# A hybrid decoder layer: the memory queries of the second token half by pair, and the memory splits ahead of the token scaling

## The chip, the cores and the metric

The kernel runs on one core of one Trainium2 chip. The metric is the device time of one execution in microseconds. PE is the TensorE, ACT the ScalarE, DVE the VectorE, POOL the GpSimd, and SP the SyncE, which here only issues DMAs. Each engine works through its own queue in order.

## The reference

One decoder layer for 1024 tokens of width 1024, all in float32:

```python
h = rmsnorm(x, norm_g)
pool_v, pool_gate, sb_q, sb_k, sb_v, sb_gate, mem_q, mem_gate = split(h @ w_in)
y_pool = pool_mixer(pool_v, pool_w, pool_scale) * silu(pool_gate)      # 256 wide
y_sb = stick_breaking_attention(sb_q, sb_k, sb_v) * silu(sb_gate)      # 8 heads of 64
mem_k, mem_v = split(rmsnorm(mem, mem_norm_g) @ w_mem_kv)              # 256 memory tokens
y_mem = memory_attention(mem_q, mem_k, mem_v) * silu(mem_gate)         # 4 heads of 64
out = x + concat(y_pool, y_sb, y_mem) @ w_out

def memory_attention(q, mem_k, mem_v):
    q, mem_k = rmsnorm(q, q_norm_g), rmsnorm(mem_k, k_norm_g)          # per head
    p = softmax(q @ mem_k.T * 64 ** -0.5)
    return p @ mem_v
```

## The kernel before

Every float32 operand of a matmul is held as a high part (a copy in a shorter format, made by ACT) and a low part (the rest, a subtraction on DVE or POOL), and each product is three matmuls: high by high, high by low, low by high. The normalised tokens, transposed, are `hh[k]` and `hl[k]` for eight blocks k of 128 channels; a projection of 128 output columns (a unit) takes eight steps of three 128x512 matmuls for each half of the tokens (th 0 and 1), so 16 steps. Its weights (512 KB) come into the one raw buffer `wr`, ACT makes the high part (L148), POOL the low part in four pieces (L152), and the two buffers `wh` and `wl` hold two units' weights each. The next unit's weights are asked for at the first step of a unit (`chain`, L227).

PE's order is the program's order throughout. Up to `start.close()` (L923) the order on ACT, DVE and POOL is the program's order too; behind it a planner in the compiler orders these three, by its own cost estimates. SP's order is the planner's everywhere.

The start. The memory (256 tokens, tiles `mt`) and its key/value weights come first. `m_evac(kk)` splits two blocks of the transposed memory, `kv_split(kk)` splits a quarter of the key/value weights, half of the low part on DVE and half on POOL (L158), and `kv_step(kk)` multiplies them on PE. Between them lie the first four token tiles: `square` on ACT, `root` (an operation on DVE and a power on POOL, L123), `newton` and `scale` on DVE (L127 to L133). `mn[i].root()` is the same for the two memory tiles, whose scales are needed only later, by `kv_evac`. `warm` issues transposes that nobody reads. `h_step(th, k)` then transposes block k of four token tiles on PE and splits it into `hh[k]` on ACT (L381) and `hl[k]` on DVE (L382).

The memory queries (two units, pr 0 and 1, of two heads each) are the first units. `half[pr, th]` are the eight steps of one half. Half 0 of both pairs runs step by step in turn, together with the last `h_step`s; then comes half 0 of the first stick-breaking query unit `u_q[0]`, with the evacuations `mq_late` of the memory queries between its steps; then half 1 of both pairs, in turn. In this last block also lie: `kv_root` and `kv_newton`, which normalise the memory keys into `kmn` (squares on ACT, a sum on DVE, a power on POOL, four small operations and two products on DVE); `mem_ss(pr, th)`, which sums the squares of the queries by head on PE (L551, 128x2 results) and copies them out on DVE; `mem_scale(th)`, which makes of them the queries' scale factors (with a power of 16 columns on POOL, L95); and `km_step(kmn, pr)`, which transposes the keys on PE (L469) and splits them into `km`, four copies on ACT (L476) and four differences on DVE (L481).

An evacuation of a query unit is two copies on ACT and two differences on DVE (L256 to L259); a memory query unit has a third ACT operation, the squares (L543).

Behind `start.close()` PE runs half 1 of `u_q[0]` and the first step of the key unit `u_k[0]`, and then `weave`, which lays the steps of memory attention (`mem_main`) between the steps of the following units by estimated costs. One item of `mem_main` is: scores on PE (L574, bank `z`), row maximum and its scaling on DVE (L576, L580), two exponentials on ACT (L584), reciprocal on DVE, scaling half on POOL and half on DVE (L595), transposes (L493) and the product with the values (L512) on PE. `weave` runs again for the four stick-breaking attentions, and the output projection ends the kernel.

A value unit (`v_unit`) evacuates each half into the one buffer `vt` (ACT L295, DVE L298), and `late(th)` transposes it on PE (L306) and splits it into `V_v`. `chain` puts `late(0)` among the unit's own steps, and `late(1)` among those of the next unit.

Of the kernel before, what the change touches and what calls it, by code (L numbers as in the profile page):

```python
# [17 lines left out]
KD = D // P  # L18
# [7 lines left out]
def layer_kernel(  # L26
# [31 lines left out]
    def ps(tag, name):  # L58
        return psum.tile([P, 512], F32, tag=tag, name=name, bufs=banks[tag])
# [75 lines left out]
    def load_raw(src, name, raw=None):  # L135
        raw = slot("wr", f"wr_{name}") if raw is None else raw
        nc.sync.dma_start(raw[:], src)
        return raw
# [26 lines left out]
    def run(steps):  # L165
        for _, fn in steps:
            fn()
# [59 lines left out]
    def chain(units, after=None):  # L227
        steps, rest = [], []
        for n, u in enumerate(units):
            nxt = units[n + 1] if n + 1 < len(units) else after  # L230
            a = list(u.steps)
            if nxt is not None:
                a[0] = (KC, lambda f0=a[0][1], nxt=nxt: (f0(), nxt.weights()))
            if u.late is not None:
                a = a[:10] + u.late(0) + a[10:]
            steps += a[:2] + rest + a[2:]
            rest = u.late(1) if u.late is not None else []
        return steps + rest

# [102 lines left out]
    mn = [Norm(mt[i][:], f"m{i}") for i in range(2)]  # L342
# [6 lines left out]
    def warm(dst, n):  # L349
        for i in range(n):  # L350
            nc.tensor.transpose(dst[:, 0:P], ident[:], ident[:])
# [38 lines left out]
    def m_evac(kk):  # L390
        tps = [(2 * kk + j, tm[kk][:, j * M : (j + 1) * M]) for j in range(2)]
        for k, tp in tps:
            nc.scalar.activation(mh[:, k, :], tp, AF.Identity, scale=gcol[:, 8 + k : 9 + k])
        for k, tp in tps:
            nc.vector.scalar_tensor_tensor(
                ml[:, k, :], tp, gcol[:, 8 + k : 9 + k], f(mh[:, k, :]), op0=ALU.mult, op1=ALU.subtract
            )
# [3 lines left out]
    def kv_split(kk):  # L401
        tags = (("wh", "wl"), ("wh", "wl"), ("qa0", "qb0"), ("KA0",))[kk]
        w_kv.append(split_w(raw_kv[kk], f"kv{kk}", tags, (nc.vector, nc.gpsimd)))

    def kv_step(kk):
        wh, wl = w_kv[kk]
        for j in range(2):
            k = 2 * kk + j
            wc = slice(j * 512, (j + 1) * 512)
            for w, m in ((wh, mh), (wh, ml), (wl, mh)):  # L410
                for i in range(2):
                    nc.tensor.matmul(
                        kvp[i][:],
                        m[:, k, i * P : (i + 1) * P],
                        w[:, wc],
                        start=(k == 0 and m is mh and w is wh),
                        stop=(k == KD - 1 and w is wl),
                    )

    kvs, kmn, k_root = [], [], []  # L420
# [134 lines left out]
    def mem_scale(th):  # L555
        c = slice(16 * th, 16 * th + 16)
        r = rsqrt_cols(ssb[:, c], 16, 1.0 / HD, f"q{th}")()
        nc.vector.tensor_scalar_mul(qsc[:, c], r[:], HD**-0.5)
# [245 lines left out]
    m_evac(0)  # L804
    kv_split(0)
    m_evac(1)
    for i in range(2):
        mn[i].root()
    kv_step(0)
    xn[0].square()  # L810
    xn[0].root()
    kv_split(1)
    xn[0].newton()
    xn[0].scale(nc.vector)
    m_evac(2)
    kv_step(1)
    xn[1].square()
    xn[1].root()
    kv_split(2)
    xn[1].newton()  # L820
    xn[1].scale(nc.vector)
    xn[2].square()
    xn[2].root()
    m_evac(3)
    kv_step(2)
    kv_split(3)
    xn[2].newton()
    xn[3].square()
    xn[3].root()
    xn[2].scale(nc.vector)  # L830
    kv_step(3)
    raw_mq = [load_raw(w_in_v[:, :, 2560 + pr * P : 2560 + (pr + 1) * P], f"mq{pr}", early_raw[4 + pr]) for pr in range(2)]
    for i in range(4, 8):
        nc.sync.dma_start(xt[i][:], xv[i * P : (i + 1) * P, :])
    xn[3].newton()
    xn[3].scale(nc.vector, slice(0, 512))
    warm(ps("tr", "warm"), 8)
    w_mq = [(slot("wh", f"wh_mq{pr}", dt=F32R), slot("wl", f"wl_mq{pr}", dt=F32R)) for pr in range(2)]
    wc = (slice(0, 512), slice(512, 1024))

# [3 lines left out]
    def mq_low(pr, c, eng):  # L844
# [7 lines left out]
    mq_low(1, wc[0], nc.gpsimd)  # L852
    mq = [mem_q(pr) for pr in range(2)]
    half = {
        (pr, th): unit_half(lambda pr=pr: w_mq[pr], f"mq{pr}", th, mq[pr][1], late_h=False) for pr in range(2) for th in range(2)
    }
    h_step(0, 0)
    mq_high(1, wc[1])
# [51 lines left out]
            mq_late[pr][n]()  # L910
    for k in range(KD):
        half[0, 1][k][1]()
        half[1, 1][k][1]()
        if k == 0:
            kv_root()
            kv_newton()
        if k in (2, 3):
            mem_ss(k - 2, 0)
        if k == 4:
            mem_scale(0)  # L920
        if k in (5, 6):
            km_step(kmn, k - 5)
    start.close()  # L923
    fill = u_q[0].steps[8:] + chain([u_k[0], u_v[0], u_v[1], u_g[0], u_q[1], u_k[1], u_g[1]], u_q[2])
    cut = 8 + 16 + 17 + 17 + 16
    fill, fill_0 = fill[:cut], fill[cut:]
    run(fill[:9])
    y_mem = [slot(f"Y{pr}", f"y_mem{pr}") for pr in range(2)]

    def mem_late(n):  # L930
        mem_ss(n, 1)
        if n == 1:
            mem_scale(1)

    fill[13:13] = [(0.45, lambda: mem_late(0))]
    fill[16:16] = [(0.45, lambda: mem_late(1))]
    weave(mem_main(mq, y_mem), fill[9:], 4, 1.0)

    def attn(p):
# [225 lines left out]
```

## Time and profile before

| | |
|---|---|
| time, median of 3 runs (lowest to highest) | 532.24 us (531.69 to 532.82) |
| the profiled execution: its time, its span | 533.07 us, 531.3 us |
| PE busy | 515.5 us, 97% of the span |
| DVE, ACT, POOL busy | 392.6, 286.7, 178.9 us (74, 54, 34%) |
| DMA | 37.25 MB, mean 70 GB/s |
| mean granted clock of PE | 0.99 |

The span goes from the first to the last instruction of the one profiled execution; all times of rows are microseconds from its start. Idle time of an engine counts only where PE comes to wait for it. The granted clock is told as a share of the full level: 1.00 is 2.4 GHz and 0.5 is 1.2 GHz.

### The profile page before, as it was taken

To read this page: it belongs to the slowest core of one execution; us is meant where nothing else is said; L and a number is where in the kernel's file an instruction comes from. 1 tells how busy PE (TensorE), PEld (TensorE's weight loads), DVE (VectorE), ACT (ScalarE), POOL (GpSimd) and SP (SyncE) were. 2 spreads that over 40 slices of the span, in tenths; PEclk is the share of its full clock that TensorE was granted. 3 is DMA by queue.
4 is the path that set the end of the run, shared out by engine and by line. 5 is a ranking of instruction groups with operands and counts; after the bars stand their busy time and mean duration, and the time that the engine had idled before them with its cause. 6 is when DMAs were issued, how large, how long until landed. Compare 5 with 4: busy or idle time off the path is not lost.

```text
span 531.3 us, 7462 instructions
## 1 busy us (share of the span) xinstructions
PE 515.5 (97%) x2724; PEld 431.9 (81%) x2724; DVE 392.6 (74%) x635; ACT 286.7 (54%) x549; POOL 178.9 (34%) x196
## 2 busy tenths in 40 slices
PE   7899979999999999999999999999999999999997
PEld 6587858888788888888888888888788888888886
DVE  3877555776667885877666777657988859999973
ACT  7687454766756555555545654545544539462400
POOL 4770445542322021022202211222345920034790
PEclk9999987999999999999999999999999999999999
DMA  8911012310110230113011113100110415413123
GB/s 316 320 44 41 0 41 74 86 35 6 41 39 1 80 81 0 41 49 93 20 39 41 41 40 80 39 16 26 41 41 0 159 42 197 159 41 119 40 110 128
DMA packets 37244, 37.25 MB, mean 70 GB/s; under 512 B 1990, under 2 KB 26840, under 8 KB 37208
## 3 DMA queue, kind: packets, MB, share of 16 engines
q1 hardware_dynamic: 37208, 36.78, 22.1%
q8 instruction: 21, 0.34, 0.3%
q14 instruction: 15, 0.12, 0.1%
HBM read 28.39 MB, written 4.19 MB: 61 GB/s over the span
## 4 chain that ended last, share of the span: by engine, by line
PE 83%; DVE 6%; ACT 5%; issue 2%; DMA 2%; POOL 1%; SPq 0%; DVEq 0%; ACTq 0%; POOLq 0%
PE av L512 7%; PE z L640 6%; PE ta L493 6%; PE u_g L209 5%; PE u_k L209 5%; PE u_v L209 5%; PE u_q L209 4%; PE u_mg L209 3%; PE oS L1047 3%; PE oS L1049 3%; PE u_g L206 3%; PE oS L1048 3%; PE u_pv L209 3%; PE u_k L206 3%; PE u_v L206 3%; PE u_mq L209 2%
## 5 line engine op out<-in xcount | busy, mean ns | idle before, releaser
L648 DVE TENSOR_TENSOR_SCAN be<-be,later 128x128 f32<-128x128 f32 (+3 forms) x64 | 92.1, 1454 | 14.4 <-ACT be L644 13.5
L498 ACT ACTIVATE ah<-ta,mone 128x512 fp32r<-128x512 f32 (+1 forms) x80 | 51.6, 645 | 58.3 <-PE ta L493 57.5
L499 DVE SCALAR_TENSOR_TENSOR al<-ta,ah 128x512 fp32r<-128x512 f32 (+1 forms) x80 | 50.7, 633 | 24.6 <-ACT ah L498 23.8
L644 ACT ACTIVATE be<-z 128x128 f32<-128x128 f32 (+3 forms) x96 | 45.5, 490 | 31.0 <-PE z L640 29.4
L493 PE MATMUL ta<-ident,be 128*128 128x128 f32 x288 | 44.9, 273 | 0.1
L493 PEld LDWEIGHTS ta<-ident,be 128*128 128x128 f32 x288 | 34.9, 140 | 8.0 <-DVE be L648 0.7
L512 PEld LDWEIGHTS av<-ah,V_v 128*128 128x128 f32 x160 | 29.7, 188 | 6.7
L512 PE MATMUL av<-al,V_v 128*128 128x256 f32 (+1 forms) x160 | 31.7, 280 | 1.1 <-DVE al L499 1.1
L512 PE MATMUL av<-ah,V_v 128*128 128x256 f32 (+1 forms) x160 | 30.3, 271 | 0.0
L152 POOL TENSOR_TENSOR wl_k<-wr_k,wh_k 128x256 fp32r<-128x256 f32 x16 | 12.0, 784 | 50.9 <-ACT wh_k L148 50.9
L206 PE MATMUL u_g<-hh,wh_g 128*128 128x512 f32 x64 | 27.8, 435 | 0.0
L206 PE MATMUL u_k<-hh,wh_k 128*128 128x512 f32 x64 | 27.6, 431 | 0.0
L206 PE MATMUL u_v<-hh,wh_v 128*128 128x512 f32 x64 | 27.1, 423 | 0.0
L152 POOL TENSOR_TENSOR wl_g<-wr_g,wh_g 128x256 fp32r<-128x256 f32 x16 | 11.3, 738 | 45.2 <-ACT wh_g L148 30.1
L209 PE MATMUL u_k<-hh,wl_k 128*128 128x512 f32 x64 | 26.3, 411 | 0.1
L209 PE MATMUL u_k<-hl,wh_k 128*128 128x512 f32 x64 | 26.2, 409 | 0.0
L1047 PE MATMUL oS<-bs,hh 128*128 128x512 f32 (+1 forms) x68 | 25.9, 381 | 0.0
L1049 PE MATMUL oS<-bs,hl 128*128 128x512 f32 (+1 forms) x68 | 25.8, 379 | 0.0
L1048 PE MATMUL oS<-bs,hh 128*128 128x512 f32 (+1 forms) x68 | 25.6, 376 | 0.0
L209 PE MATMUL u_v<-hl,wh_v 128*128 128x512 f32 x64 | 25.3, 396 | 0.0
L595 POOL TENSOR_SCALAR pe_m<-pe_m,nb_m 128x256 f32<-128x256 f32 x16 | 16.5, 1031 | 26.2 <-DVE nb_m L592 21.0
L209 PE MATMUL u_g<-hl,wh_g 128*128 128x512 f32 x64 | 25.3, 395 | 0.0
(312 smaller groups left out, 1486.8 us busy)
## 6 DMA issues: line engine op xcount, KB each, us to landing
x<-in_x_dram SPq DMA_DIRECT2D x8, 512.0 KB, 5.6
wr_q<-in_w_in_dram SPq DMA_DIRECT2D x4, 512.0 KB, 4.4
wr_k<-in_w_in_dram SPq DMA_DIRECT2D x4, 512.0 KB, 3.7
wr_v<-in_w_in_dram SPq DMA_DIRECT2D x4, 512.0 KB
KA_k<-KA_k SPq DMA_DIRECT2D x8, 256.0 KB, 5.5
KB_k<-KB_k SPq DMA_DIRECT2D x8, 256.0 KB, 4.5
wr_g<-in_w_in_dram SPq DMA_DIRECT2D x4, 512.0 KB, 4.3
xr<-in_x_dram SPq DMA_DIRECT2D x8, 256.0 KB, 4.6
```

Source lines behind the costliest of these rows:

```text
L206: nc.tensor.matmul(pt[:], wh[:, kc], hh[k][:, c], start=(k == 0), stop=False)
L209: nc.tensor.matmul(pt[:], w[:, kc], h[k][:, c], start=False, stop=(k == KD - 1 and n == 1))
L493: nc.tensor.transpose(tp[:, o : o + P], src, ident[:])
L498: nc.scalar.activation(ah[:, :w], tp[:, :w], AF.Identity, bias=mone[:, 0:1])
L499: nc.vector.scalar_tensor_tensor(al[:, :w], tp[:, :w], -1.0, f(ah[:, :w]), op0=ALU.add, op1=ALU.subtract)
L512: nc.tensor.matmul(av[:, 256 - bw : 256], vs[n], part[:, o : o + bw], start=(first and part is ah and n == 0), stop=(last and part is al a ...
L640: nc.tensor.matmul(zp[:, 0:w], q[h][:, tcol], k[h][:, n, s0 : s0 + w], start=(n == 0), stop=(n == 1))
L644: nc.scalar.activation(be[:, s0 : s0 + w], zp[:, 0:w], AF.Sigmoid, scale=-(HD**-0.5))
L648: nc.vector.tensor_tensor_scan(be[:, rev], be[:, rev], mask, 1.0, op0=ALU.mult, op1=ALU.max)
L1047: nc.tensor.matmul(bk[:, c], xh[:, tcol], wh[:, c], start=(n == 0), stop=False)
L1048: nc.tensor.matmul(bk[:, c], xh[:, tcol], wl[:, c], start=False, stop=False)
L1049: nc.tensor.matmul(bk[:, c], xl[:, tcol], wh[:, c], start=False, stop=(n == 3))
```

## The change

In the block of half 1, pair 0 does its eight steps first and then pair 1 its eight. The key transposes move from the joint steps 5 and 6 to the steps 6 and 7 of pair 0. The weights of `u_k[0]` are asked for at step 1 of pair 1, so that their split stands in the fixed order of ACT and POOL. The sums of the second half's query squares move out of the weave: `mem_ss(0, 1)` into pair 1's step 5, `mem_ss(1, 1)` and `mem_scale(1)` behind the fourth step of `u_q[0]`'s half 1.

At the start, `m_evac`, `kv_split` and `kv_step` move ahead of the scaling of the token tiles, and the two roots of the memory behind it. Four warm-up transposes stand where there were eight.

For half 0 of the memory queries (`late_h`) the low part of the weights is multiplied second and the low part of the tokens third; before it was the other way round.

In `chain`, `late(0)` stands behind 13 steps of a value unit, not 10, and `late(1)` behind 5 steps of the next unit, not 2.

```diff
@@ chain
-                a = a[:10] + u.late(0) + a[10:]
-            steps += a[:2] + rest + a[2:]
+                a = a[:13] + u.late(0) + a[13:]
+            steps += a[:5] + rest + a[5:]
@@ the start
     m_evac(1)
-    for i in range(2):
-        mn[i].root()
     kv_step(0)
+    m_evac(2)
     xn[0].square()
+    kv_split(1)
+    kv_step(1)
+    m_evac(3)
     xn[0].root()
-    kv_split(1)
+    xn[1].square()
+    kv_split(2)
     xn[0].newton()
     xn[0].scale(nc.vector)
-    m_evac(2)
-    kv_step(1)
-    xn[1].square()
+    kv_step(2)
     xn[1].root()
-    kv_split(2)
+    xn[2].square()
+    kv_split(3)
     xn[1].newton()
     xn[1].scale(nc.vector)
-    xn[2].square()
     xn[2].root()
-    m_evac(3)
-    kv_step(2)
-    kv_split(3)
+    xn[3].square()
     xn[2].newton()
-    xn[3].square()
     xn[3].root()
     xn[2].scale(nc.vector)
     kv_step(3)
+    for i in range(2):
+        mn[i].root()
...
-    warm(ps("tr", "warm"), 8)
+    warm(ps("tr", "warm"), 4)
...
-        (pr, th): unit_half(..., mq[pr][1], late_h=False) for pr in range(2) for th in range(2)
+        (pr, th): unit_half(..., mq[pr][1], late_h=(th == 0)) for pr in range(2) for th in range(2)
@@ the block of half 1
     for k in range(KD):
         half[0, 1][k][1]()
-        half[1, 1][k][1]()
         if k == 0:
             kv_root()
             kv_newton()
         if k in (2, 3):
             mem_ss(k - 2, 0)
         if k == 4:
             mem_scale(0)
-        if k in (5, 6):
-            km_step(kmn, k - 5)
+        if k in (6, 7):
+            km_step(kmn, k - 6)
+    for k in range(KD):
+        half[1, 1][k][1]()
+        if k == 1:
+            u_k[0].weights()
+        if k == 5:
+            mem_ss(0, 1)
     start.close()
...
-    run(fill[:9])
+    run(fill[:4])
+    mem_ss(1, 1)
+    mem_scale(1)
+    run(fill[4:9])
...
-    def mem_late(n):
-        mem_ss(n, 1)
-        if n == 1:
-            mem_scale(1)
-
-    fill[13:13] = [(0.45, lambda: mem_late(0))]
-    fill[16:16] = [(0.45, lambda: mem_late(1))]
```

## Rows read from the trace of the kernel before

**Rows 1.** The page's busy line of PE, and its line of the clock that PE was granted, in 40 slices of 13.3 us (tenths of full speed).

```profile
PE 515.5 (97%) x2724; PEld 431.9 (81%) x2724; DVE 392.6 (74%) x635; ACT 286.7 (54%) x549; POOL 178.9 (34%) x196
PEclk9999987999999999999999999999999999999999
```

**Rows 2.** Whom PE waited for over the whole span: total us, number of waits, longest us.

```profile
PE z_m L574 <- ACT pe_m L584: 3.3, 1, 3.3
...
PE tv_v L306 <- DVE vt_v L298: 1.5, 2, 1.1
PE kv L412 <- DVE w_kv L158: 1.3, 1, 1.3
...
PE u_mq L206 <- DVE G_mq L259: 0.5, 1, 0.5
PE av L512 <- DVE al_m L504: 0.4, 1, 0.4
```

**Rows 3.** Four stretches around the longest wait: the stretch, its length, busy us (and instructions) of PE, PE's weight loads, DVE, ACT and POOL, then the granted clock, the DMA's share and GB/s.

```profile
69.84:74.53 4.69, 4.69 (x29) 4.06 (x27) 2.92 (x5) 0.10 (x1) 1.69 (x3) 1.00 0.36 107
74.53:77.85 3.32, 0.00 (x1) 0.00 (x0) 0.25 (x3) 2.31 (x6) 1.20 (x2) 0.84 0.04 12
77.85:87.14 9.29, 9.29 (x32) 8.03 (x33) 3.81 (x13) 2.83 (x9) 7.08 (x7) 0.51 0.20 56
87.14:97.00 9.86, 9.86 (x60) 8.49 (x59) 6.98 (x20) 7.54 (x19) 4.32 (x6) 1.00 0.21 53
```

**Rows 4.** ACT's instructions in order of time (start, duration, line, tile, and in brackets the idle time before and what ended it).

```profile
60.17 3.86 ACT L476 ACTIVATE km<-tk,gcol 64x256 fp32r<-64x256 f32 x8 [8.61 <-PE tk L469]
...
67.58 1.06 ACT L148 ACTIVATE wh_k<-wr_k 128x1024 fp32r<-128x1024 f32 x1
...
75.52 1.06 ACT L148 ACTIVATE wh_v<-wr_v 128x1024 fp32r<-128x1024 f32 x1 [5.58 <-DMA wr_v<-in_w_in_dram]
76.60 0.56 ACT L584 ACTIVATE pe_m<-z_m,nb_m,qsc 128x256 f32<-128x256 f32 x1
```

**Rows 5.** In order of time, what the other queues did for the same weights and scores: two requests of SP (SPq), the low part of the key weights on POOL, and on DVE the first scaled row maximum.

```profile
40.08 0.38 SPq L137 DMA_DIRECT2D wr_k<-in_w_in_dram  x1
...
68.72 2.81 POOL L152 TENSOR_TENSOR wl_k<-wr_k,wh_k 128x256 fp32r<-128x256 f32 x4 [7.76 <-ACT wh_k L148]
...
71.56 8.32 SPq L137 DMA_DIRECT2D wr_v<-in_w_in_dram  x2
72.12 0.16 DVE L580 TENSOR_TENSOR nb_m<-nb_m,qsc 128x2 f32<-128x2 f32 x1
```

**Rows 6.** Pieces of the chain of work that ended last (start, length, engine, tile, line): one `mem_ss`, then a key step and a `mem_ss` behind the longest wait, then a key step further on.

```profile
53.88 0.79 PE sp L551 x8
...
79.08 0.43 PE u_k L206
79.50 0.85 PE u_k L209 x2
...
81.64 1.50 PE sp L551 x8
...
87.39 0.24 PE u_k L206
87.62 0.46 PE u_k L209 x2
```

**Rows 7.** PE in order of time: the first matmul of the block of half 1, and two matmuls of the first key step.

```profile
48.80 0.39 PE L206 MATMUL u_mq<-hh,wh_mq 128*128 128x512 f32 x1
...
69.03 0.40 PE L209 MATMUL u_k<-hl,wh_k 128*128 128x512 f32 x1
69.50 0.50 PE L209 MATMUL u_k<-hh,wl_k 128*128 128x512 f32 x1
```

**Rows 8.** DVE and POOL in order of time: the sum, the power and the products of the memory keys' norm, the power of the queries' scale, and the key differences.

```profile
52.23 0.69 DVE L436 TENSOR_REDUCE ssk<-kmn 128x8 f32<-128x512 f32 x1
...
53.20 1.66 POOL L95 TENSOR_TENSOR r_k<-v_k,mhalf 128x8 f32<-128x8 f32 x1 [13.15 <-DVE v_k L94]
...
56.73 0.76 DVE L447 TENSOR_TENSOR kmn<-kvs,r_k 128x256 f32<-128x256 f32 x2
...
58.05 2.90 POOL L95 TENSOR_TENSOR r_q<-v_q,mhalf 128x16 f32<-128x16 f32 x1 [1.78 <-DVE v_q L94]
...
62.12 3.97 DVE L481 SCALAR_TENSOR_TENSOR km<-tk,gcol,km 64x256 fp32r<-64x256 f32 x8
```

**Rows 9.** The start in order of time: on DVE the last memory split and the scales of the third and (half) the fourth token tile, on POOL the fourth tile's power and two low parts of the query weights, and on PE the last matmul of the first round of both pairs.

```profile
19.43 1.73 DVE L158 TENSOR_TENSOR w_kv<-raw,w_kv 128x512 fp32r<-128x512 f32 x1
...
21.57 0.81 DVE L133 TENSOR_SCALAR x<-x,ss_x 128x1024 f32<-128x1024 f32 x1
...
21.67 1.11 POOL L123 TENSOR_TENSOR ss_x<-ss_x,mhalf 128x1 f32<-128x1 f32 x1 [1.06 <-DVE ss_x L122]
22.76 1.28 POOL L846 TENSOR_TENSOR wl_mq<-raw,wh_mq 128x512 fp32r<-128x512 f32 x1
...
23.32 1.00 DVE L133 TENSOR_SCALAR x<-x,ss_x 128x512 f32<-128x512 f32 x1
...
24.00 1.45 POOL L846 TENSOR_TENSOR wl_mq<-wr_mq,wh_mq 128x512 fp32r<-128x512 f32 x1
...
27.31 0.40 PE L209 MATMUL u_mq<-hh,wl_mq 128*128 128x512 f32 x1
```

More of the change, by code (lines that the diff above doesn't have):

```diff
@@ L854, in layer_kernel @@
     half = {
-        (pr, th): unit_half(lambda pr=pr: w_mq[pr], f"mq{pr}", th, mq[pr][1], late_h=False) for pr in range(2) for th in range(2)
+        (pr, th): unit_half(lambda pr=pr: w_mq[pr], f"mq{pr}", th, mq[pr][1], late_h=(th == 0)) for pr in range(2) for th in range(2)
     }
```

## The prediction

> **What bounds the kernel now.** I read the page's busy times and the clock line first, then who PE waited for, then the stretches around the longest wait, and last the queues of ACT, POOL, DVE and SP there. PE is busy for 97% of the span, and the granted clock is full except in two slices out of forty, around 66 to 93 us [rows 1]. So what PE does in order sets the end, and a microsecond can only be gained where PE idles or runs at the lower clock. Its waits are few: one of 3.3 us on the exponentials of memory attention, 1.5 us in two waits on a value tile, 1.3 us near the start, and two below 0.5 [rows 2]. The 3.3 us costs more than itself. PE stands still from 74.53 to 77.85, and from 77.85 to 87.14 it works at a granted clock of 0.51, the 1.2 GHz level; before and behind it stands 1.00, the 2.4 GHz level [rows 3].
>
> Why PE stood still is read from the other queues. The key weights `wr_k` were asked for at 40.08, but their high part `wh_k` is made by ACT only at 67.58, behind eight copies for the memory keys (from 60.17) and both pairs' query evacuations. POOL's four low parts follow from 68.72 to 71.53. They free the one raw buffer, so the value weights `wr_v` are asked for at 71.56, and ACT, in order, holds at `wh_v` for 5.58 us until they land at 75.5. Behind it in ACT's queue stand the exponentials, whose factor DVE had begun to write at 72.12 [rows 4, 5]. They start at 76.60, and PE, which needs their bank, at 77.85.
>
> **The block of the second token half.** Before, both pairs advance together from 48.80 to 62.94, so both weight buffers `wh`/`wl` stay in use until 62.9. In sequence, pair 0 ends early and frees its buffer for the key weights.
>
> I place the new order on the old clock. A step of three matmuls is 0.24 + 0.46 = 0.70 us, one `mem_ss` 0.79 [rows 6]. From 48.80 [rows 7], seven steps and two `mem_ss` bring PE to the first key transposes at 48.80 + 4.9 + 1.6 = 55.3. The keys are not ready then. DVE reduces their squares at 52.23, POOL raises to the power until 54.86, DVE normalises the two tiles until 57.49 [rows 8]. Nothing in the diff moves that chain, so PE waits for the first tile (about 57.1) and then the second: 57.5 less 55.3 less the transposes, some 2.0 us. That is the **added wait: +2.0**, bounds 1.4 (the keys 0.6 earlier) and 2.6. Behind it stand pair 0's last step and then all of pair 1; who waits for those is ACT with the query evacuations.
>
> ACT then makes four key copies, pair 0's three evacuations and four more key copies, which from the old rows (3.86 for the eight, 0.6 each for the three) end at 57.7 + 3.9 + 1.8 = 63.4, and `wh_k` ends at 64.5. POOL's low parts take 2.81, so `wr_v` is asked for near 67.4 instead of 71.56 and lands about 3.9 later, at 71.3. DVE's eight key differences (3.97) and four query differences (0.69 each) start behind the scale factors at 62 and are through by 69 [rows 8]. PE meanwhile does pair 1 (5.6), one `mem_ss`, the eight query steps, the other `mem_ss` and one key step, from 58.8 to about 72.4. The first scores follow; their exponentials can start 2.3 later (old: scores 69.84, factor 72.12), near 74.7. `wh_v` is off ACT by 72.4. So the value weights come 2.3 us ahead of the exponentials instead of 3 us behind. **The wait goes: -3.3.** **The low clock goes with it: -4.4.** In that stretch a step took 0.43 + 0.85 = 1.28 against 0.70 and `mem_ss` 1.50 against 0.79 [rows 6], which gives 45 to 47% of 9.29 us, 4.2 to 4.4; by the granted clock it is 0.49 x 9.29 = 4.55 [rows 3].
>
> Two smaller waits go too. Pair 1's first matmul waited 0.49 for the bank of pair 1's old query half [rows 2]; eight steps later that bank is long free: **-0.5**. The third matmul of the first key step started 0.47 after the second (69.03 to 69.50) where 0.23 is usual, behind the low part of the key weights [rows 7]; that is now ready by 67.4 and needed at 71.6: **-0.2**. The two `mem_ss` of the second half are only moved, out of the weave into and behind the block, so they cost nothing as long as their squares are ready. Pair 1's squares are due on ACT at about 67.2 and PE asks at 68.0. If that cover is gone, the cost is the difference, under 1 us.
>
> **The transposes of values** go three steps further from the evacuation they need, about 2.1 us of PE work. The two waits were 1.5 together and the longer 1.1 [rows 2], both shorter than that: **-1.5**, bounds -1.1 and -1.5. Later readers of the values stand more than ten steps away.
>
> **The start.** Four warm-up transposes fewer are 0.4 us on PE, but the fourth token tile is due at about the same time, so the chains decide. In the old order DVE's half of the last memory split ran 1.73 us (from 19.43), the third tile's scale followed at 21.57, the fourth tile's half scale ended at 24.32 [rows 9]. Put ahead, that split no longer waits behind two scales and an evacuation; I follow DVE with the old durations. The split ends at 18.0, the second tile's scale (up to 1.3) at 19.6, the third tile's power at 20.2 and scale at 21.6, the fourth's power (1.11 again) at 21.9 and its half scale between 22.8 and 23.4. That is 0.9 to 1.5 earlier. POOL gives some back: the two roots of memory now stand in front of the low parts of the query weights, which start at 23.2 instead of 22.76 and end at 24.5 and 25.9 (1.28 and 1.45). With the low part now second of the three matmuls, PE waits for it twice, but the round ends about 26.4 instead of 27.5. **Start: -1.1**, bounds 0 (POOL eats all of it) and -1.6 (the token chain alone).
>
> **The sum.** -3.3 - 4.4 - 0.5 - 0.2 - 1.5 - 1.1 + 2.0 = -9.0. The weave is planned anew without two of its entries; I add 0.5 for one more small wait like that of 0.41 on `al_m` [rows 2]: -8.5. The profiled execution took 533.07 (span 531.3 and 1.8 around it): 524.6. It lies 0.83 over the median of the runs, 532.24, so on their scale 523.7.
>
> **A rule against the change.** The sum adds waits of PE: 2.0 before the keys and a few short ones at the start. The waits of that kind in the old trace, up to 1.3 us [rows 2], left the granted clock in its slices full [rows 1]; the clock fell once, in the wait of 3.32, whose mean of 0.84 means that its last 1.06 us were at the low level, so 2.26 after PE had stopped [rows 3]. The Trainium skill, TensorE: Matmul & The Clock Gate, section "A second HAM failure mode: psum-queue depth-cycling", warns that PE's frequent small idles between groups of matmuls make the clock swing. By that rule the result would be the first rival, 528.1; by the rows it is 523.7.
>
> **Rivals.**
> *The clock falls in the new wait.* The wait stands at 55.3 and lasts 2.0, with two transposes of 0.1 in it. One low stretch is worth 4.4: 523.7 + 4.4 = 528.1. For it: 2.0 is close to the 2.26 after which it fell. Against: dense matmuls stand directly before the new wait, while `mem_ss`, whose matmuls move two columns, stood before the old one.
>
> *The exponentials wait all the same.* Behind the block the order on ACT is the planner's, and it put `wh_v` in front once. If the value weights land 2.3 us later than I reckon, the exponentials wait again, and with 3.3 more than that the old price is back: 523.7 + 7.7 = 531.4. For it: the planner's order cannot be seen. Against: POOL's low parts and so the request are now inside the fixed order.
>
> *The keys come much later (slower than before).* All of the gain is used up when the wait for the keys is 2.0 + 8.5 - 4.4 = 6.1 us and takes the clock along, that is with the keys after 61.6. With a wait of 7.5 it gives 523.7 + 5.5 + 4.4 = 533.6. It would take DVE or POOL holding the key chain 4 us longer. The longest piece there, the 16-column power of 2.90, stands behind the keys [rows 8], so it is unlikely.
>
> **Chances.** Forecast 0.68 (its own range 521.5 to 526), clock 0.13, exponentials 0.11, keys 0.05, no effect at all 0.03. From 521 to 530 lies 0.81 of this plus a part of the third case. This kernel's runs differ by about 0.2%, so 0.2% is what a measurement can tell from no change: faster takes the first two, and half of the third, 0.86; same 0.06; slower 0.08.
>
> **What would show it.** `wh_k` on ACT near 63 and not after 67; `wr_v` asked for near 67 to 68 less the start's gain; no wait of PE on the exponentials and a clock of 1.00 from 62 to 90; a new wait of about 2 us of PE on the normalised keys near 55; no `tv_v` waits; the first token transposes a microsecond earlier. Wrong would be: a clock of 0.5 anywhere before 90, a wait of ACT on the value weights, or a key wait above 3 us.

## The result, and the profile after

The changed kernel takes 528.3 us (median of 20 runs, 526.93 to 532.71) against 532.64 for the kernel before on the same chip (531.53 to 533.3). The ratio is 0.9943, with a 95% interval of 0.9923 to 0.9964; it goes by the means, 529.4 against 532.4. It is faster, by 3.0 us in the means, about a third of the 8.5 forecast, and by 4.3 in the medians, half of it. 528.3 lies between 521 and 530, but outside the forecast's own range of 521.5 to 526; the value forecast was 523.7, and below 526.9 no execution came.

Each execution has its own mean granted clock: of the changed kernel's twenty, seven have 0.999 to 1.00 and take 526.9 to 527.9 us, seven have 0.990 and take 531.6 to 532.7, and six have a clock between (527.1 to 531.0), while the kernel before had 0.989 to 0.997 in all of 24 executions of a later comparison.

The profiled execution is one of the long ones (532.06 us, span 530.3 against 531.3). Its busy line and clock line, which answer to [rows 1]:

```profile
PE 515.0 (97%) x2720; PEld 433.1 (82%) x2720; DVE 393.3 (74%) x635; ACT 287.2 (54%) x549; POOL 177.0 (33%) x196
PEclk9999899999899999999999999999999999999999
```

PE is as busy as before. The dip over two slices (8 and 7) has become two single eights further apart; a third low stretch, at 25 us, is split over two slices and doesn't show there. Whom PE waited for (total us, number, longest), to be read against [rows 2]:

```profile
PE z_m L574 <- ACT pe_m L584: 2.1, 1, 2.1
PE ta_m L493 <- DVE al_m L504: 1.9, 1, 1.9
PE tk L469 <- DVE kmn L447: 1.6, 1, 1.6
PE tx L379 <- DVE x L133: 1.2, 1, 1.2
PE tx L379 <- DVE ss_m L122: 1.1, 1, 1.1
```

The wait on `pe_m` went from 3.3 to 2.1 and did not vanish. `tv_v`, `u_mq` and the 1.3 on `w_kv` near the start are gone from the list; the waits on `ta_m`, the keys (`tk`) and two on the first token tiles are new. The stretches with these waits and what follows them (columns as in [rows 3]; the clock is the third number from the end):

```profile
21.00:25.15 4.15, 1.91 (x15) 1.49 (x14) 2.37 (x9) 1.59 (x3) 3.51 (x5) 1.00 1.01 399
25.15:28.56 3.41, 3.41 (x12) 2.58 (x11) 2.96 (x5) 3.41 (x7) 3.41 (x4) 0.50 0.08 26
56.55:58.14 1.59, 0.01 (x2) 0.01 (x1) 1.47 (x5) 0.00 (x0) 0.65 (x1) 1.00 0.00 0
58.14:62.69 4.55, 4.54 (x14) 3.54 (x15) 1.36 (x8) 3.68 (x8) 2.91 (x1) 0.63 0.00 0
79.40:81.49 2.09, 0.00 (x2) 0.00 (x1) 1.47 (x5) 1.26 (x5) 0.00 (x0) 1.00 0.62 187
135.10:137.04 1.94, 0.01 (x1) 0.04 (x1) 1.30 (x4) 1.92 (x6) 1.07 (x1) 1.00 0.11 33
137.04:141.20 4.16, 4.16 (x17) 3.64 (x18) 2.07 (x4) 2.71 (x5) 0.01 (x1) 0.59 0.00 0
```

Three times PE fell to the 1.2 GHz level after it had stood idle or half idle: 25.15 to 28.56 at 0.50, and within 58.14 to 62.69 and 137.04 to 141.20. By (1 - clock) x length these are 1.7 + 1.7 + 1.7 = 5.1 us. The first two lie before 90, which the prediction had named as a sign of being wrong. The longest wait, 2.09, has none behind it. Before it was one stretch of 9.29 [rows 3].

The queues that feed the first exponentials (ACT, POOL, DVE and SP's request in order of time, to be read against [rows 4, 5, 8]):

```profile
61.92 0.17 DVE L98 TENSOR_TENSOR t_q<-r_q 128x16 f32<-128x16 f32 x1 [3.02 <-POOL r_q L95]
...
64.61 1.06 ACT L148 ACTIVATE wh_k<-wr_k 128x1024 fp32r<-128x1024 f32 x1
...
68.60 0.37 SPq L137 DMA_DIRECT2D wr_v<-in_w_in_dram  x1
71.85 2.90 POOL L95 TENSOR_TENSOR r_q<-v_q,mhalf 128x16 f32<-128x16 f32 x1 [3.28 <-DVE v_q L94]
72.24 1.06 ACT L148 ACTIVATE wh_v<-wr_v 128x1024 fp32r<-128x1024 f32 x1 [2.62 <-DMA wr_v<-in_w_in_dram]
74.72 2.84 POOL L152 TENSOR_TENSOR wl_v<-wr_v,wh_v 128x256 fp32r<-128x256 f32 x4
74.78 0.70 DVE L98 TENSOR_TENSOR t_q<-r_q 128x16 f32<-128x16 f32 x1 [3.01 <-POOL r_q L95]
...
77.61 0.18 DVE L558 TENSOR_SCALAR qsc<-r_q 128x16 f32<-128x16 f32 x1
77.81 0.68 DVE L258 TENSOR_TENSOR qa_q<-u_q,qa_q 64x512 fp32r<-64x512 f32 x1
...
79.23 0.69 DVE L576 TENSOR_REDUCE nb_m<-z_m 128x2 f32<-128x512 f32 x1
...
80.23 0.56 ACT L584 ACTIVATE pe_m<-z_m,nb_m,qsc 128x256 f32<-128x256 f32 x1 [4.73 <-DVE nb_m L580]
```

The weights come earlier, as was forecast: `wr_v` is asked for at 68.60 instead of 71.56, and `wh_v` no longer stands directly in front of the exponentials. ACT still waits 2.62 for `wr_v` (5.58 before [rows 4]), which the prediction had named as a sign of being wrong. What stands in front of the exponentials is `mem_scale(1)`. Its power occupies POOL for 2.90 us, DVE holds for 3.01 behind it, and then four of the five operations that follow take 0.66 to 0.70 each, where they took 0.17 to 0.18 from 61.92 on. The query differences and the first maximum queue behind them on DVE. The exponentials start at 80.23.

One pair of points sorts the whole time: PE's first matmul of the block and its first token score (`z` of L640). The kernel before, then after:

```profile
148.50 0.34 PE L640 MATMUL z<-KA_k,qa_q 128*128 128x128 f32 x2
```

```profile
49.71 0.39 PE L206 MATMUL u_mq<-hh,wh_mq 128*128 128x512 f32 x1
...
147.40 0.34 PE L640 MATMUL z<-KA_k,qa_q 128*128 128x128 f32 x2
```

Up to the block it is 0.9 later (49.71 against 48.80 [rows 7]); from the block to the first token score 97.69 against 99.70, 2.0 shorter; behind it 382.9 against 382.8. `chain` also moves the transposes of the value units of later weaves, but the stage behind 148 us is the same to 0.1 us, so the experiments are compared by the first two stages.

### The profile page after: what moved, and what is told of

It reads as the page before. It is cut to its first block, busy times and chain, and to the rows that moved or that the text cites. A ratio compares the mean times of both kernels' runs of the same rounds, so it can differ in the third digit from the quotient of the medians.

```text
span 530.3 us, 7458 instructions
## 1 busy us (share of the span) xinstructions
PE 515.0 (97%) x2720; PEld 433.1 (82%) x2720; DVE 393.3 (74%) x635; ACT 287.2 (54%) x549; POOL 177.0 (33%) x196
## 4 chain that ended last, share of the span: by engine, by line
PE 85%; DVE 7%; ACT 2%; DMA 2%; POOL 2%; issue 1%; SPq 0%; ACTq 0%; POOLq 0%
PE av L512 8%; PE z L640 7%; PE ta L493 6%; PE u_g L209 6%; PE u_v L209 6%; PE u_k L209 5%; PE u_q L209 5%; PE u_g L206 3%; PE u_v L206 3%; PE u_mg L209 3%; PE oS L1047 3%; PE oS L1049 3%; PE u_pv L209 3%; PE oS L1048 3%; PE u_k L206 2%; PE u_q L206 2%
## 5 line engine op out<-in xcount | busy, mean ns | idle before, releaser
L584 ACT ACTIVATE pe_m<-z_m,nb_m,qsc 128x256 f32<-128x256 f32 x32 | 17.8, 561 | 18.6 <-DVE nb_m L580 15.1
L206 PE MATMUL u_k<-hh,wh_k 128*128 128x512 f32 x64 | 26.5, 414 | 0.0
L209 PE MATMUL u_g<-hh,wl_g 128*128 128x512 f32 x64 | 25.7, 402 | 0.0
```

The source lines that it names most:

```text
L206: nc.tensor.matmul(pt[:], wh[:, kc], hh[k][:, c], start=(k == 0), stop=False)
L209: nc.tensor.matmul(pt[:], w[:, kc], h[k][:, c], start=False, stop=(k == KD - 1 and n == 1))
```

## The experiments

Each time is a median, in brackets the lowest and the highest; each ratio, with its 95% interval, is against the kernel before on the same chip. "Full clock" means a mean of 0.999 or 1.00 in that execution.

**mem_scale back into the weave.** Everything else as in the change.

```
-    run(fill[:4])
-    mem_ss(1, 1)
-    mem_scale(1)
-    run(fill[4:9])
+    run(fill[:9])
+
+    def mem_late():
+        mem_ss(1, 1)
+        mem_scale(1)
+
+    fill[15:15] = [(0.45, mem_late)]
```

> The changed kernel with mem_ss(1, 1) and mem_scale(1) put back into the weave, at about their old place. Theory of the moved scale factors: in the changed kernel DVE stands in the factors' four small operations from 74.8 to 77.6, because POOL's 16-column power ends at 74.75 and POOL's value split then slows them, and the first scores (74.8) are read only at 79.2; so PE's wait of 2.09 us at 79.4 goes, and the time falls by about 2 us, from a median of 528.3 to about 526.3. Rival: the factors hold DVE just as long inside the weave (they held it 1.6 us in the old kernel), or the wait is the exponentials' own; then the time stays at 528 and the wait only moves.

Measured: 530.59, ratio 0.9982 (0.9967 to 0.9996). A miss. The exponentials did start earlier (76.67) and PE's wait there fell to 1.16, but seven executions at full clock took 529.9 to 530.8, 3 us more than the change at full clock. Taking `mem_scale` away from that place alone doesn't help; the run called the fourth corner below shows why for the old start.

**The value transposes at their old steps** (10 and 2 instead of 13 and 5).

```
-                a = a[:13] + u.late(0) + a[13:]
-            steps += a[:5] + rest + a[5:]
+                a = a[:10] + u.late(0) + a[10:]
+            steps += a[:2] + rest + a[2:]
```

> The changed kernel with the value transposes at their old places (10 and 2 instead of 13 and 5). Theory of the taken bank: the wait of 1.94 us at 137 on transposed probabilities comes from the last value transpose, which now falls between two of them and takes one of the two banks they share; with the old place it goes, and the two old waits on value tiles (1.5 together) come back: about 0.5 faster, 527.8. Rival: the 1.94 is the planner's order on ACT and DVE and has nothing to do with the transposes; then it stays, and the time grows by 1.5 to 529.8.

Measured: 529.4, ratio 0.9945 (0.992 to 0.9969), the same as the change. In PE's waits `z_m` (2.1) and the keys (1.6) stand as in the change, and there is again:

```profile
...
PE tv_v L306 <- DVE vt_v L298: 1.6, 1, 1.6
```

The 1.9 on `ta_m` is gone and 1.6 on `tv_v` is back. So the -1.5 was earned and paid again. In the changed kernel's trace the second half's transposes (133.32) stand between two `ta_m` (132.89 and 137.03). Both take their PSUM tiles from the tag `tr`, which has two, so the later `ta_m` gets the tile that the earlier one still holds. PE in the changed kernel:

```profile
132.89 0.60 PE L493 MATMUL ta_m<-ident,pe_m 128*128 128x128 f32 x4
133.32 0.60 PE L306 MATMUL tv_v<-ident,vt_v 128*128 128x128 f32 x4
...
137.03 0.41 PE L493 MATMUL ta_m<-ident,pe_m 128*128 128x128 f32 x2 [1.94 <-DVE al_m L504]
```

**The old start**, block and transposes as changed. The whole order from the memory splits to the query weights is that of before; a part of the edit:

```
+    for i in range(2):
+        mn[i].root()
     kv_step(0)
-    m_evac(2)
     xn[0].square()
-    kv_split(1)
-    kv_step(1)
-    m_evac(3)
     xn[0].root()
...
-    warm(ps("tr", "warm"), 4)
+    warm(ps("tr", "warm"), 8)
```

> The changed kernel with the old order of the start (memory splits between the token scales, memory roots early, eight warm-up transposes); late_h stays as changed. Theory of the start: the new order is worth 0.8 us where the clock holds, and its waits at 21.8 and 23.2 bring a low clock from 25.1 to 28.6 in some executions; with the old order the shortest times grow by 0.8 (527.0 to 527.8) and the executions near 532 become fewer, so the median is 527.8 to 528.5. Rival: the executions near 532 come from the waits behind it, at 58 and 137; then they stay as frequent as they were (8 of 20) and the median grows to about 529.

Measured: 528.02 (527.07 to 529.02), ratio 0.9921 (0.9908 to 0.9934). At full clock 527.1 to 528.1, as the change at full clock; but of its six runs none took more than 529.02, and none had a clock below 0.996. The new start gives no time (the theory's 0.8 didn't show). Executions near 532 came with it in 8 of 20 and without it in 0 of 6, which points to it and is too few to show it.

**The keys later**, behind pair 1's second and third step.

```
         half[0, 1][k][1]()
...
-        if k in (6, 7):
-            km_step(kmn, k - 6)
...
         half[1, 1][k][1]()
...
+        if k in (1, 2):
+            km_step(kmn, k - 1)
```

> The changed kernel with the key transposes at steps 1 and 2 of pair 1 instead of steps 6 and 7 of pair 0. Theory of the wait for the keys: PE reaches them after 58.1, when they are ready, so the wait of 1.58 us and the low clock behind it (59.3 to 62.7, worth 1.7) go: 1.6 us less in the best executions (525.4) and about 2 less in the median (526.3). Rival: the keys' copies on ACT and differences on DVE then end later and the first scores or the scale factors wait for them; then the wait moves to 79 and the time stays at 528.

Measured: 531.11, ratio 0.9978 (0.9966 to 0.9989). Worse than the theory and the rival, and none of the eleven executions had full clock (0.986 to 0.993). The key wait is gone and so is the one on `z_m`, but PE waits 3.7 on `sp` instead (`sp` from DVE's `ssb`), in `mem_ss` ahead of the weave. DVE copies each `ssb` in order, behind eight key differences of 0.5 which now come later. The wait moved.

**The kernel before, once more**, with no edit, to see another execution of it.

> The kernel before, unchanged, to see where its low-clock stretches stand in another execution. Theory A (the forecast's term: PE at the low clock behind the exponentials is what sets the time there, 0.43 us lost per us at 1.2 GHz): an execution with one low stretch of 3.4 us instead of three is 3.0 us shorter. Theory B (PE is ahead of its suppliers there, so the low clock mostly fills time in which it would wait): it is only about 1.0 us shorter, and PE shows waits of 1 to 2 us between 78 and 92 that the first profile didn't have. If this execution has three low stretches again, nothing is told apart: 532 to 533, the wait of 3.3 in its place.

This one had a mean clock of 0.997. Three stretches of it (the second begins where the clock fell, inside the wait), and its waits:

```profile
74.38:77.40 3.02, 0.00 (x1) 0.00 (x0) 0.25 (x3) 2.31 (x6) 1.20 (x2) 0.92 0.05 13
76.91:80.33 3.42, 2.93 (x9) 2.54 (x10) 2.18 (x6) 2.20 (x9) 3.42 (x6) 0.50 0.03 8
...
88.69:89.67 0.98, 0.01 (x1) 0.00 (x0) 0.95 (x3) 0.00 (x0) 0.00 (x0) 1.00 0.11 29
```

```profile
PE z_m L574 <- ACT pe_m L584: 3.0, 1, 3.0
...
PE av L512 <- DVE al_m L504: 1.5, 2, 1.0
```

The same wait of 3.0 was followed by 3.4 us at the low level and not by 10.2 (the first profile: 76.78 to 87.02). The span is 529.3 against 531.3: 6.8 us less at the low level gave 2.0, where 0.47 per us would give 3.2. About 1.0 came back as a new wait at 88.69. Over the 24 runs of the kernel before in the first comparison it is less still: twelve with 0.996 or 0.997 have a median of 531.7, eight with 0.989 or 0.990 one of 532.8, 1.1 apart. The 2.0 of the two profiles lies midway between the theories; the new wait is theory B's, and so is the 1.1 of the 24 runs.

**The block alone**: the old start and the old transposes (10 and 2) of the experiments above, in one kernel.

> Only the block of the second half and what moves with it (mem_ss and mem_scale of pair 1 behind it, low part second); the start's old order with 8 warm-up transposes, and the value transposes at their old places. Theory (all of the gain is the block's; start and transposes bring 0 each): 528, as with the old start alone (528.0); PE waits of about 1.6 on the keys, 1.0 on z_m, 1.5 on the value transposes and none on ta_m. Rival (the value transposes did bring their 1.5): 529.5.

Measured: 527.12 (526.63 to 527.26, all at full clock), ratio 0.9906 (0.9888 to 0.9924). Its DVE beside POOL, which shows the price of `mem_scale` there:

```profile
71.96 0.17 DVE L99 TENSOR_TENSOR t_q<-t_q,v_q 128x16 f32<-128x16 f32 x1
72.17 0.64 DVE L100 TENSOR_SCALAR t_q<-t_q 128x16 f32<-128x16 f32 x1
72.85 0.66 DVE L101 TENSOR_TENSOR r_q<-r_q,t_q 128x16 f32<-128x16 f32 x1
```

```profile
72.04 2.83 POOL L152 TENSOR_TENSOR wl_v<-wr_v,wh_v 128x256 fp32r<-128x256 f32 x4 [0.32 <-ACT wh_v L148]
```

The operation ahead of POOL's 72.04 takes 0.17, those beside it 0.64 and 0.66. PE's two points are 48.23 and 142.10: from the block to the first token score 93.87, against 99.70 before and 97.69 in the profile of the change. The block alone is all of the gain: its ratio, 0.9906, is no worse than the 0.9943 of the whole change.

**The second half's transposes at four steps**, old start.

```
-            steps += a[:5] + rest + a[5:]
+            steps += a[:4] + rest + a[4:]
```

> Old start order, the block as changed, and the second half's value transposes four steps into the next unit instead of five or two. Theory (five steps put them between two ta_m and take the bank the second one needs, two steps put them ahead of their evacuation): neither the wait of 1.6 on tv_v nor that of 1.9 on ta_m, 528.0 - 1.9 = 526.1 at full clock. Rival (the tail of the weave is bound by DVE's and ACT's chain, PE waits there wherever the transposes stand): 527.5 to 528, with 1.5 to 2 us of PE's waits on ta_m or av between 128 and 140.

Measured: 527.05 (525.47 to 529.39), ratio 0.991 (0.9875 to 0.9944). At full clock 525.5 and 526.4, as the theory said (526.1); the profile has 0.4 on `tv_v` and nothing on `ta_m`. Two of four executions had a lower clock, 0.997 and 0.994, with 527.8 and 529.4, although the start was old and the wait on `ta_m` gone. So over all runs it is not separated from the block alone (527.12).

**Keys in pair 1's first two steps, mem_scale in the weave, transposes at four, old start.** The same kernel ran twice, in two comparisons. To the run with the transposes at four it adds `mem_late` in the weave, as in the first experiment, and this:

```
-        if k in (6, 7):
-            km_step(kmn, k - 6)
...
+        if k in (0, 1):
+            km_step(kmn, k)
```

> As the run with the transposes at four, and the two key steps go into pair 1's first two steps (1.4 us of work ahead of the first), mem_ss and mem_scale of pair 1 back into the weave. Theory (each wait has its own place and goes when its cause goes): no key wait above 0.4, no wait on mem_ss, the exponentials not before 75: 526.1 - 1.3 = 524.8. Rival (the chain that feeds the first exponentials is ACT's and DVE's, from the key copies to wh_v and the query differences, so PE waits at z_m for whatever it saved before): 526 to 527, with the key wait's 1.3 us found again at z_m.

> The version with old start, keys in pair 1's first two steps, mem_ss and mem_scale in the weave and transposes at four, once more, beside the three others on one chip: 525.3 (525.1 to 525.5), all at full clock. If it shows low-clock runs here, its lead over the change is by chance of the clock: 527 to 528.

Measured: 525.33 (525.14 to 525.41), ratio 0.9873 (0.9852 to 0.9894), and 525.28 (524.79 to 525.58), 0.9874 (0.986 to 0.9889); all eight at full clock. ACT and SP in the second, with the same lines as after:

```profile
58.17 1.91 ACT L476 ACTIVATE km<-tk,gcol 64x256 fp32r<-64x256 f32 x4
60.10 1.06 ACT L148 ACTIVATE wh_k<-wr_k 128x1024 fp32r<-128x1024 f32 x1
61.19 1.92 ACT L476 ACTIVATE km<-tk,gcol 64x256 fp32r<-64x256 f32 x4
64.08 8.12 SPq L137 DMA_DIRECT2D wr_v<-in_w_in_dram  x2
67.82 1.06 ACT L148 ACTIVATE wh_v<-wr_v 128x1024 fp32r<-128x1024 f32 x1 [1.98 <-DMA wr_v<-in_w_in_dram]
...
73.54 0.57 ACT L584 ACTIVATE pe_m<-z_m,nb_m,qsc 128x256 f32<-128x256 f32 x1 [2.72 <-DVE nb_m L580]
```

The high part of the key weights now stands between the two groups of key copies, 4.5 us earlier than in the change; `wr_v` follows at 64.08 and `wh_v` at 67.82, ahead of the evacuation of `u_q[0]`'s half 1; the exponentials start at 73.54, and PE doesn't wait for them at all. What waits are left in the block and behind it are 1.7 on `al_m` and 0.2 on the keys. The theory's 524.8 had no wait on `al_m`.

**The same with the new start**, then with 16 warm-up transposes instead of 4.

```
-    warm(ps("tr", "warm"), 4)
+    warm(ps("tr", "warm"), 16)
```

> The version with the keys in pair 1's first two steps, mem_ss and mem_scale of pair 1 in the weave and the transposes at four, now with the start of the change (memory splits ahead, 4 warm-up transposes). Theory (the new start gives no time, because the token tiles' chain ends when it did, and brings executions with low-clock stretches): at full clock 525.3 as without it, and some runs 1.5 to 5 longer, so a median of 526 to 528. Rival A (the forecast's start term): 524.2, with the first token transposes 1.1 earlier. Rival B (the low stretches came from the key wait and the ta_m wait, not from the start): all runs at full clock, 525.3.

Measured: 525.61 (525.16 to 526.05), ratio 0.9881 (0.9867 to 0.9896): two executions at full clock with 525.2, as with the old start, and two with a clock of 0.996 and 0.997, 526.0, less above the others than the theory's 1.5. In the profile of one of those one low stretch is again behind the waits for the token tiles:

```profile
21.43:24.23 2.80, 0.64 (x5) 0.45 (x5) 2.04 (x8) 0.09 (x1) 2.56 (x4) 1.00 1.01 405
24.23:27.65 3.42, 3.42 (x14) 3.03 (x12) 2.64 (x4) 3.37 (x7) 3.42 (x3) 0.50 0.29 108
```

> The same with 16 warm-up transposes instead of 4, which take 1.3 us of the time in which PE waits for the second and third token tile anyway. Theory (PE's idling between 21.8 and 24.3 is what brings the low stretches): full clock in most runs, 525.3 to 525.6. Rival (the low stretches follow from the order of DVE and POOL, or from the waits later on): the same mix as with 4, median 526 to 528; or, if the transposes are in the way, 526.0 at full clock.

Measured: 525.08 (524.95 to 525.15), ratio 0.9871 (0.9856 to 0.9886), all four at full clock. It is the fastest kernel here, 1.3% under the kernel before, though its lead on the old start is 0.2 us and not separated. With the idle time there filled, none of four executions has the low stretch, against two of four without; that may still be chance.

**mem_scale in front, keys late.** The version at 525.3, with `mem_late` taken out of the weave and `run(fill[:4])`, `mem_ss(1, 1)`, `mem_scale(1)`, `run(fill[4:9])` as in the change.

> Old start, keys in pair 1's first two steps, transposes at four, and mem_ss and mem_scale of pair 1 at the change's place, ahead of the weave. It differs from the best version by that alone. Theory (mem_scale there holds DVE behind POOL's power of 2.9 us, and with it the query differences and the first max; PE also waits for the squares): first exponentials 2.5 to 3.5 later than in the best version, PE waits of 1.5 to 3 in sum on sp and z_m, 527 to 528. Rival (the key copies were what mattered): 525.3 to 525.6.

Measured: 528.98 (528.72 to 529.16), ratio 0.9943 (0.9926 to 0.996), 3.7 more than the best version on the same chip. The first exponentials came at 80.36, 6.8 later, for PE itself stood 3.0 on `sp` (66.68) and then had 6.8 us at the low level. The wait is that of the moved `mem_ss`, behind the key differences on DVE, as in the run with the keys later; all four executions were below full clock.

**mem_scale in the weave, keys early**, the fourth corner: the version at 525.3, with `if k in (6, 7): km_step(kmn, k - 6)` in pair 0's loop as in the change.

> Old start, keys where the change has them (pair 0's last two steps), transposes at four, mem_ss and mem_scale of pair 1 in the weave: the fourth corner beside the runs with the keys early and mem_scale in front (526 at full clock), keys late and mem_scale in front (529.0), keys late and mem_scale in the weave (525.3). Theory (mem_scale's place and the keys' place add up: the key wait costs 1.3 to 1.6): 526.6 to 527. Rival A (mem_scale in the weave costs time with the keys early, as the run with the new start, 530.1 at full clock, said): 528.5 to 529.5, with a PE wait of 2 or more between 80 and 100 on pair 1's exponentials. Rival B (only the later keys make room for the chain to the exponentials): 527.5 to 528, wait at z_m of 1 to 2.

Measured: 528.5 (527.42 to 528.6), ratio 0.9927 (0.9904 to 0.995). It is rival A's time without rival A's wait: no PE wait between 80 and 100 reaches 2, and `z_m` has rival B's 1.3. ACT shows why the two places don't add up:

```profile
64.42 1.06 ACT L148 ACTIVATE wh_k<-wr_k 128x1024 fp32r<-128x1024 f32 x1
72.18 1.06 ACT L148 ACTIVATE wh_v<-wr_v 128x1024 fp32r<-128x1024 f32 x1 [4.33 <-DMA wr_v<-in_w_in_dram]
73.15 0.58 ACT L256 ACTIVATE qa_q<-u_q 64x512 fp32r<-64x512 f32 x1
76.78 0.56 ACT L584 ACTIVATE pe_m<-z_m,nb_m,qsc 128x256 f32<-128x256 f32 x1 [2.46 <-DVE nb_m L580]
```

With the keys early, `wh_k` stands behind all eight key copies, so `wh_v` comes at 72.18 and holds the query evacuation, whose differences stand on DVE in front of the first maximum. PE's waits behind the block:

```profile
PE av L512 <- DVE al_m L504: 1.7, 2, 1.3
...
PE z_m L574 <- ACT pe_m L584: 1.3, 1, 1.3
```

The 1.3 on `z_m` and the key wait of 1.6 are what separates this run from the best version: from the block to the first token score it needs 94.45, the best 91.84. The 1.7 on `al_m` (1.3 of it at 87.71), behind `mem_scale` in the weave, stands in both. It is what `mem_scale` costs there; with `mem_scale` in front there is no wait on `al_m`. The four corners side by side, all with the old start and the transposes at four (the exponentials count from PE's first matmul of the block):

| keys | mem_scale | time, us | first exponentials | PE waits in and behind the block |
|---|---|---|---|---|
| pair 0's end | in front | 525.5 and 526.4 (full clock), median 527.05 | 28.4 | keys 1.6, `z_m` 1.5, `tv_v` 0.4 |
| pair 0's end | in the weave | 528.5 | 27.3 | keys 1.6, `z_m` 1.3, `al_m` 1.7 |
| pair 1's start | in front | 528.98 (none at full clock) | 31.6 | keys 0.2, `sp` 3.0, `tv_v` 0.4 |
| pair 1's start | in the weave | 525.3 | 24.7 | keys 0.2, `al_m` 1.7 |

## Why the prediction was wrong, point by point

**The block's terms came out, taken together, and in part by chance.** -3.3 - 4.4 - 0.5 - 0.2 + 2.0 and the 0.5 for a small wait are -5.9 on the profiled execution. The block alone at full clock gave 93.87 - 99.70 = -5.8. But 99.70 is from an execution with 10.2 us at the low level; against the other profile of the kernel before, with 3.4 us, it is 93.87 - 97.88 = -4.0, and by the means of that comparison (527.0 and 532.1) -5.1. Singly: the key wait was 1.6 and not 2.0; the wait for the bank (0.49) and the one in the first key step are gone; the request for `wr_v` came at 68.60 and not near 67.4, 0.9 of it because the block itself began 0.9 later. The wait for the exponentials was not -3.3: 1.5 of it stays in the block alone, 2.1 in the change.

**The step that failed there** is the start of the exponentials "near 74.7", from which "The wait goes: -3.3" follows. The prediction followed the value weights on ACT up to them, and of the two moved `mem_ss` it asked only whether their squares are ready, "so they cost nothing". It didn't follow DVE, which must take the first maximum before them, and two things hold that up. One is `mem_scale(1)`, which follows the `mem_ss`: a POOL power of 2.90 and five DVE operations, which in the old order stood behind the first exponentials and now stand ahead of the maximum in DVE's queue. The other is `wh_v` on ACT ahead of the query copies, and so ahead of the query differences on DVE. "Near 74.7" became 76.64 in the block alone and 80.23 in the profiled execution of the change, where, behind the low stretch within 58.14 to 62.69, four of the operations fell beside POOL's `wl_v`.

The four corners show that removing one of the two is not enough. With `mem_scale` back in the weave and `wh_v` still in front, the exponentials come only 1.1 earlier (28.4 to 27.3), `z_m` still has 1.3, `al_m` gets 1.7, and the time rises by 2 to 3 us. With the keys later, which brings `wh_v` out of the way, and `mem_scale` in front, PE waits 3.0 in the moved `mem_ss`. Only with both out of the way do the exponentials start 3.7 earlier and PE's wait on them go. So what held up the change is not `mem_scale`'s place by itself, but that place and the keys' together.

On the slowing of the small operations the Trainium skill, SBUF — State Buffer, section "Who interferes with whom", says that a DVE instruction with two inputs in SBUF contends with a GpSimd instruction that reads it. The trace agrees for those with two inputs: 0.17 to 0.18 without POOL, 0.66 to 0.70 beside it. Those with one input (L100, L558) took as long beside POOL, 0.64 to 0.66, which that sentence alone would not give.

**The transposes, -1.5, came to about 0.** The waits on `tv_v` went, and 1.9 on `ta_m` came. The step that failed looked at how far the transposes stand from their evacuation and from their readers, not at whose tile they take. At four steps both waits are nearly gone (0.4 on `tv_v`): 525.5 and 526.4 at full clock against 527.1 to 528.1 with five and 526.6 to 527.3 at the old places. These are two executions; over all runs the gain isn't clear.

**The start, -1.1, came to 0,** the lower bound given. PE's first query step of the token tiles starts at 25.45 after and 25.48 before: the 1.3 on the last memory split is gone, and PE waits for the third and the fourth tile instead (1.1 + 1.2). DVE's last split and three scales:

```profile
17.81 0.69 DVE L158 TENSOR_TENSOR w_kv<-raw,w_kv 128x512 fp32r<-128x512 f32 x1
...
19.47 1.28 DVE L133 TENSOR_SCALAR x<-x,ss_x 128x1024 f32<-128x1024 f32 x1
...
21.49 0.27 DVE L127 TENSOR_SCALAR ss_x<-ss_x 128x1 f32<-128x1 f32 x1 [0.67 <-POOL ss_x L123]
...
21.99 0.81 DVE L133 TENSOR_SCALAR x<-x,ss_x 128x1024 f32<-128x1024 f32 x1
...
23.74 0.55 DVE L133 TENSOR_SCALAR x<-x,ss_x 128x512 f32<-128x512 f32 x1
```

The split ends at 18.5 (said: 18.0), the scales at 20.8, 22.8 and 24.3 (said: 19.6, 21.6 and 22.8 to 23.4; in the old order the last was 24.32 [rows 9]). The tiles run in a circle from DVE to POOL's power and back, and DVE stands before each Newton step (0.67 here); I had counted the old durations without the places where one engine waits for the other.

**The clock: low stretches that the sum didn't have.** The sum took the low clock off and put none in its place, but 13 of the 20 executions of the change are below full clock. The first rival gave 528.1 for one low stretch of 4.4 behind the key wait. That 528.3 is so near is chance: the rival counts on 523.7 for the rest, which didn't come, and the profiled execution has three stretches of 3.4 us, others none. The prediction weighed a rule of the Trainium skill, TensorE: Matmul & The Clock Gate, section "A second HAM failure mode: psum-queue depth-cycling", that frequent small idles make the clock swing. The trace agrees in part: low stretches stand behind waits of 1.6 and 1.9 and behind two of 1.1 and 1.2, but none behind the 2.09 of the same execution, nor behind 1.6 and 2.0 in the profile of the old start. The argument from [rows 1, 2], that waits up to 1.3 left the clock full, was a reading of one execution.

**The price of the clock was half right.** In the changed kernel it nearly held: between its executions at full clock (527.3) and those at 0.990 (531.9) lie 4.6 us, 0.45 per us if each of the latter has 10.2 us at the low level like the profiled one. Behind the exponentials of the kernel before it gave 0.29 (2.0 for 6.8 us), and over its runs 0.16 (1.1 for 6.8 us); the new wait at 88.69 shows one place where PE, sooner there, waits for DVE instead.

So the difference of 4.6 between 523.7 and 528.3 is made of the transposes and the start (2.6) and, in the median, low stretches (527.3, the median of the seven runs at full clock, against 528.3). About 1 is left. A part may be that the low clock of the kernel before was counted from one of its long executions (-5.9 there, -5.1 by the means above); that is argued and not shown.

**What stays open:** why one execution has the low stretches and another of the same kernel not. In the two pairs that differ by the start alone, executions below full clock are 13 of 20 with the new start and 2 of 6 with the old, and 2 of 4 and 0 of 8; that points to the start, but two of four had them at the old start with the transposes at four. Why `mem_scale` in the weave with the new start needed 529.9 even at full clock is seen only in the run that differs from it by the old start and the transposes at four; its own profile is of an execution at 0.990.

## What to carry to other kernels

When an operation is moved, follow everything that it issues behind itself, on each engine's queue, up to the work on the critical path: here two small matmul groups brought a 2.9 us power on one engine and five small operations on another. Where two causes hold the same work, change each alone and both together: here each alone lost time, and both together gained it. Before a short wait is removed by moving something later, look whose buffer it will take there. Read the clock from several executions before giving it a price: one profile shows neither how often it falls nor what a fall costs.

## What was unexpected of the hardware

DVE's operations on 128x16 values take 0.17 us alone and 0.64 to 0.70 beside POOL's low parts, four times as long and about as long as one of POOL's four pieces (2.83 / 4 = 0.71). The low-clock stretches seen were 3.4, 6.8 and 10.2 us long, and the same kernel showed none, one or three of them from one execution to the next (by their mean clock where there is no profile), with medians 4.6 us apart in the changed kernel and 1.1 us in the kernel before.
